# A decoder step in split fp32: activations, gains, first-stage weights and cached keys handed over in the layouts that the kernel used to make with transposes

## The chip, the cores and the metric

One core of one Trainium2 chip runs one launch of one program. The time is the device time of a launch in microseconds (us); for this kernel a change of more than 0.2% (about 4.3 us) can be told from no change.

## What is computed

The reference is one inference step of a two-layer decoder trunk over 1024 prompt tokens and 64 sample tokens (8 sequences of 8), model width 1024, all in fp32. The part around the change:

```
def gmlp_mixer(h, n, w_in, ln_g, ln_b, w_s, b_s, w_out):   # h = rms_norm(x, sg_norm_pre)
    z = jax.nn.gelu(h @ w_in, approximate=False)
    u, v = jnp.split(z, 2, axis=-1)
    v = layer_norm(v, ln_g, ln_b)
    vc = v.reshape(B, S // n, n, SGU_GROUPS, SGU_GROUP_DIM)
    w = jnp.where(causal, w_s[:, :n, :n], 0.0)              # causal token weights, per group
    mixed = jnp.einsum('gts,bcsgd->bctgd', w, vc) + b_s[:, :n].T[:, :, None]
    y = u * mixed.reshape(B, S, SGU_WIDTH)
    return y @ w_out, v_rows
...
x = x + rms_norm(out, norm_post)                            # then a SwiGLU FFN of width 2816
...
kk = jnp.concatenate([cache_k, k_new], axis=1)              # layer 2, sample tokens: 128 cached keys each
scores = jnp.einsum('btkgd,bskd->bkgts', qg, kk)            # 16 query heads on 2 key heads, window 128, sinks
```

Layer 1 is the gated mixer and its FFN; layer 2 is sliding-window attention (prompt and sample tokens) and its FFN.

## The kernel before

Features lie on the 128 partitions and tokens on the free axis. The 1088 tokens are cut into three chunks, CH = 384, 384 and 320 columns; the 1024 features into KD = 8 tiles. Each fp32 operand is held as two halves, a rounded high part (ACT writes it) and the remainder (DVE subtracts), and a product is three matmuls, high*high, high*low and low*high (`chain`, L636 to L638): 8 tiles of the contraction by 3, 24 matmuls for one output tile and chunk.

The first stage computes v = gelu(h @ w_in[:, 1024:]), 8 weight column tiles by 3 chunks. It works as follows. SP loads x in 9 blocks of 128 tokens by rows (L583), two weight tiles into the two `raw` buffers (L472), and 14 gain and bias vectors of 8 rows each into one tile (L599). TensorE transposes every block feature tile by feature tile into PSUM (`prep_x`, L702, 72 transposes of 128x128 or 128x64), ACT and DVE split the result into the x pairs (L642, L643). The vectors are turned by two transposes (L612, L618). A weight tile is multiplied by the gain of the norm on DVE (L512, for the first tile piecewise on ACT and DVE, L518, L519), then split (L396, L397). `scale_x` squares the rows of x and sums them on ACT (L711), DVE and POOL make rsqrt of the mean (L714, L715), TensorE turns it into a row over partitions (L720), DVE copies it (L722, `srow`). A chain's result stays in one of 5 PSUM banks until the `srow` of its chunk is there (`sgate`); then DVE multiplies (L768) and ACT takes gelu (L769) into the tile `vT[d]`, POOL adds up over the features (L773). Chains of tiles d = 0, 1, 2 go first, chunk by chunk as x arrives; from d = 3 on they run tile by tile. I write (d, c) for the chain of weight tile d and chunk c.

Later stages: the causal token weights `sg_w_s` are loaded by rows, cut with a select on POOL (L820, L822) and turned on TensorE (`token_weights`, L830, L834; 8 and 8 transposes, ACT copies them out). In the attention, `Samples` loads the cached keys of a key head by rows into a `raw` buffer (L309), turns them in 8 transposes (L324) and copies them out on ACT (L326), twice.

The program is written in an order which a scheduler turns into one queue per engine; `flow` is a list of work to be written later, by a count of TensorE time. ACT and DVE are held to the written order in the first stage (`manual_schedule`). All loads wait in the one queue of SP, with at most 8 in flight, and a load into a `raw` buffer waits until DVE has read the tile before it.

## Time and profile before

| | |
|---|---|
| median of 3 runs | 2127.33 us (2126.31 to 2130.13) |
| the profiled execution, its own time | 2133.59 us |
| its span, first to last instruction | 2131.6 us |
| TensorE busy in the span | 98% |
| VectorE, ScalarE, GpSimd busy | 64%, 49%, 8% |
| mean granted TensorE clock | 0.995 of full |

The profiled execution took 6.3 us longer than the median of the runs, and 2.0 us of its time lie outside its span. TensorE is PE in the profile, VectorE DVE, ScalarE ACT, GpSimd POOL; SP issues the loads. A row of a timeline is the start in us, the length, the engine, line, operation, output and inputs, and in brackets the idle time before it and what ended that.

### The profile page before, as it was taken

Reading aid. Unit: us, or ns where it says so; the run is one execution under the profiler, and the core shown is the slowest. Engines: PE = TensorE matmul, PEld = TensorE weight load, DVE = VectorE, ACT = ScalarE, POOL = GpSimd, SP = SyncE. Lnnn points to the kernel's source line nnn. Section 1 sums busy time; section 2 is a strip of 40 time slices with the busy share of each in tenths; the row PEclk is TensorE's granted clock in tenths of the full one; section 3 lists DMA queues with packets and bytes.
Section 4 is the critical chain, followed back from the end, with each engine's and each line's share of the span. In section 5 each row is a group of like instructions: output and inputs, shape, how many; then the busy total and the mean of one; then the engine's idle time right before and its main releaser. Section 6 shows DMA issues by size and latency. Waiting matters only on the chain.

```text
span 2131.6 us, 29327 instructions
## 1 busy us (share of the span) xinstructions
PE 2098.7 (98%) x10996; PEld 1797.8 (84%) x10996; DVE 1370.7 (64%) x2205; ACT 1048.1 (49%) x2112; POOL 167.1 (8%) x226
## 2 busy tenths in 40 slices
PE   7999999999999999999999999999999999999998
PEld 6999988888888888888799887788888888888886
DVE  5456558666666666567767776486566656665676
ACT  5234547544444443434567675565444444444342
POOL 0422211000000000000013221010000000000000
PEclk9999999999999999999999999999999999999999
DMA  4211134232323237757342111332222333277574
GB/s 137 70 40 37 55 112 137 76 100 81 102 95 100 81 101 256 282 169 257 113 146 59 48 46 54 106 127 81 90 92 91 99 96 93 81 264 269 177 256 148
DMA packets 176723, 257.10 MB, mean 121 GB/s; under 512 B 24659, under 2 KB 104773, under 8 KB 176582
## 3 DMA queue, kind: packets, MB, share of 16 engines
q1 hardware_dynamic: 176582, 255.24, 37.1%
q8 instruction: 86, 1.41, 0.3%
q14 instruction: 55, 0.45, 0.1%
HBM read 188.96 MB, written 60.62 MB: 117 GB/s over the span
## 4 chain that ended last, share of the span: by engine, by line
PE 93%; DVE 4%; ACT 2%; DMA 1%; issue 0%; POOL 0%; SPq 0%; DVEq 0%; POOLq 0%; ACTq 0%
PE bank L1614 15%; PE bank L1388 13%; PE bank L1389 13%; PE bank L1390 13%; PE bank L636 5%; PE bank L638 5%; PE bank L637 5%; PE aux L1614 4%; PE bank L1020 3%; PE bank L1022 3%; PE bank L1021 3%; PE bank L1468 2%; PE bank L1467 2%; PE aux L1622 2%; PE aux L1121 1%; PE aux L2359 1%
## 5 line engine op out<-in xcount | busy, mean ns | idle before, releaser
L1388 PE MATMUL bank<-act,act 128*128 128x512 f32 x1232 | 485.0, 394 | 2.3 <-ACT act L1796 2.3
L1389 PE MATMUL bank<-act,act 128*128 128x512 f32 x1232 | 482.4, 392 | 0.0
L1390 PE MATMUL bank<-act,act 128*128 128x512 f32 x1232 | 479.7, 390 | 0.0
L1614 PE MATMUL bank<-act,act 128*128 128x512 f32 x1452 | 341.2, 389 | 0.0
L1614 PEld LDWEIGHTS bank<-act,act 128*128 128x128 f32 x1452 | 272.4, 188 | 56.5
L397 DVE TENSOR_TENSOR act<-raw,act 128x1024 fp32r<-128x1024 f32 x189 | 233.4, 1236 | 126.4 <-ACT act L396 117.3
L396 ACT ACTIVATE act<-raw 128x1024 fp32r<-128x1024 f32 x189 | 199.8, 1058 | 205.1 <-PE bank L1468 71.1
L1390 PEld LDWEIGHTS bank<-act,act 128*128 128x128 f32 x1232 | 231.4, 188 | 49.0
L1388 PEld LDWEIGHTS bank<-act,act 128*128 128x128 f32 x1232 | 231.6, 188 | 48.2 <-ACT act L1796 3.1
L1389 PEld LDWEIGHTS bank<-act,act 128*128 128x128 f32 x1232 | 231.8, 188 | 43.4
L642 ACT ACTIVATE act<-act 128x1024 fp32r<-128x1024 f32 (+4 forms) x183 | 152.7, 882 | 174.2 <-PE bank L1614 65.8
L636 PE MATMUL bank<-act,act 128*128 128x384 f32 (+1 forms) x624 | 210.9, 338 | 1.4 <-DVE act L768 1.4
L638 PE MATMUL bank<-act,act 128*128 128x384 f32 (+1 forms) x624 | 207.7, 333 | 0.3 <-DVE act L397 0.3
L637 PE MATMUL bank<-act,act 128*128 128x384 f32 (+1 forms) x624 | 206.7, 331 | 0.7 <-DVE tok L993 0.7
L643 DVE TENSOR_TENSOR act<-act,act 128x1024 fp32r<-128x1024 f32 (+4 forms) x183 | 176.6, 1005 | 35.0 <-ACT act L642 24.4
L480 ACT ACTIVATE raw<-raw,vcol 128x256 f32<-128x256 f32 x352 | 152.0, 498 | 70.3 <-DMA raw<-in_f_w_up 50.8
L998 POOL TENSOR_TENSOR tok<-tok,expo 128x1 f32<-128x1 f32 (+1 forms) x63 | 39.0, 619 | 1594.0 <-DVE tok L993 1593.9
L636 PEld LDWEIGHTS bank<-act,act 128*128 128x128 f32 x624 | 119.0, 191 | 3.6 <-DVE act L768 1.6
L637 PEld LDWEIGHTS bank<-act,act 128*128 128x128 f32 x624 | 119.0, 191 | 1.5 <-DVE tok L993 1.0
L638 PEld LDWEIGHTS bank<-act,act 128*128 128x128 f32 x624 | 118.8, 190 | 1.5 <-issue 0.9
L1020 PE MATMUL bank<-act,act 128*128 128x512 f32 x256 | 102.3, 402 | 0.8 <-ACT act L396 0.4
L1021 PE MATMUL bank<-act,act 128*128 128x512 f32 x256 | 100.9, 395 | 0.0
(298 smaller groups left out, 3160.1 us busy)
## 6 DMA issues: line engine op xcount, KB each, us to landing
act<-in_f_w_down SPq DMA_DIRECT2D x90, 512.0 KB
raw<-in_f_w_gate SPq DMA_DIRECT2D x44, 512.0 KB
raw<-in_f_w_up SPq DMA_DIRECT2D x44, 512.0 KB
act<-hid_s SPq DMA_DIRECT2D x40, 512.0 KB
rows<-stream SPq DMA_DIRECT2D x24, 512.0 KB
hid_x<-rows SPq DMA_DIRECT2D x44, 256.0 KB
hid_s<-act SPq DMA_DIRECT2D x44, 256.0 KB
hid_s<-rows SPq DMA_DIRECT2D x44, 256.0 KB
```

Of the source, the lines that this page charges most:

```text
L396: nc.scalar.activation(self.hi, raw, AF.Copy)
L397: nc.vector.tensor_tensor(self.lo, raw, self.hi.bitcast(F32), op=ALU.subtract)
L636: nc.tensor.matmul(out[:, :n], h, xh[:, cs:cs + n], start=begin, stop=False)
L637: nc.tensor.matmul(out[:, :n], h, xl[:, cs:cs + n], start=False, stop=False)
L638: nc.tensor.matmul(out[:, :n], l, xh[:, cs:cs + n], start=False, stop=end)
L643: nc.vector.tensor_tensor(lo, src, hi.bitcast(F32), op=ALU.subtract)
L1020: nc.tensor.matmul(ps[:m, :], xh, h, start=begins and j == 0, stop=False)
L1021: nc.tensor.matmul(ps[:m, :], xl, h, start=False, stop=False)
L1388: nc.tensor.matmul(ps, h, xh, start=begin and k == 0, stop=False, skip_group_check=not begin)
L1389: nc.tensor.matmul(ps, h, xl, start=False, stop=False, skip_group_check=not begin)
L1390: nc.tensor.matmul(ps, l, xh, start=False, stop=k == 3, skip_group_check=not begin)
L1614: nc.tensor.matmul(ps, x, w, start=begin and e == k == 0, stop=end and e == n - 1 and k == 2, skip_group_check=adds)
```

## The change

All five edits are in the data's layout and in the code that follows from it. The host hands over more arrays, laid out anew (`laid_out`): x by feature (`x_turned`, 1024 by 1088), `sg_w_in` as 16 column tiles that are contiguous per partition, the vectors as columns (`columns`, 128 by 106), the token weights and cached keys turned.

1. `prep_x` has no transposes: x_turned is loaded into the tiles `vT[d]` in pieces of 384 or 320 columns, and split from there. `scale_x` still needs x by rows, so x is loaded a second time; the squares overwrite it.
2. The vectors are one load; no transposes.
3. The token weights are loaded turned, and POOL's selects work on the turned tile.
4. The cached keys are loaded turned, straight into their slot, by two loads at `enter`; no `raw` buffer, no transposes, no copy.
5. The first stage has a written order that includes SP's queue: tiles d = 0 and 1 both use the piecewise preparation, interleaved with the splits of chunk 0 and chunk 1; (0, 1) and (1, 0) are written k by k together (`v_chains`); the weight tiles d = 2 and 3 are loaded into two free activation tiles (`W.first(apool)`), so that four weight tiles are on their way before a buffer comes free.

```diff
         def enter(self, slot, kc, v):
...
+            for r in range(2):
+                nc.sync.dma_start(self.kc[r * HD:(r + 1) * HD, :DB * P], a["cache_k_turned"][kv])
...
-            for hb in range(2):
-                ps = aux()
-                for b in range(4 * hb, 4 * hb + 4):
-                    nc.tensor.transpose(ps[:, b % 4 * P:(b % 4 + 1) * P], self.raw[:, b * P:(b + 1) * P], ident)
-                flow.pe(400)
-                nc.scalar.activation(self.kc[:, hb * 512:(hb + 1) * 512], ps, AF.Copy)
...
+        def first(self, pool):
+            self.raws.append(pool)
+            self.load()
...
+    def load_part(c, ds=range(KD)):
+        cs, n = CH[c]
+        for d in ds:
+            nc.sync.dma_start(vT[d][:, cs:cs + n], a["x_turned"][d * P:(d + 1) * P, cs:cs + n])
+
+    nc.sync.dma_start(vcol, a["columns"])
+    load_part(0, range(4))
+    W.first(rpool)
+    load_part(0, range(4, KD))
+    W.first(rpool)
+    load_part(1)
     for b in range(3):
         load_x(b)
...
+    W.first(apool)
+    load_part(2)
+    for b in range(3, 6):
+        load_x(b)
+    W.first(apool)
...
     def prep_x(c, ds=range(KD)):
         cs, n = CH[c]
-        blocks = blocks_of(c)
         for d in ds:
-            ps = aux()
-            for j, (b, m) in enumerate(blocks):
-                nc.tensor.transpose(ps[:, j * P:j * P + m], xt[b][:m, d * P:(d + 1) * P], ident[:m, :m])
-            split(x[d][0][:, cs:cs + n], x[d][1][:, cs:cs + n], ps[:, :n])
-        flow.pe(3 * len(ds) * 120)
+            split(*(t[:, cs:cs + n] for t in (*x[d], vT[d])))
...
+    def v_chains(*some):
+
+        pss = [bank() for _ in some]
+        for k in range(KD) if len(some) > 1 else [None]:
+            for ps, (d, c, w) in zip(pss, some):
+                chain(ps, w, x, *CH[c], **({} if k is None else dict(ks=[k], begins=k == 0, ends=k == KD - 1)))
+        for ps, (d, c, w) in zip(pss, some):
+            v_end(ps, d, c)
...
+    with tc.manual_schedule(engines={mybir.EngineType.Activation, mybir.EngineType.DVE, mybir.EngineType.SP}):
+        prep_x(0, [0])
+        W.prepare(1, lambda j: j < 7 and prep_x(0, [j + 1]))
         ww = [W.get()]
         v_chain(0, 0, ww[0])
+        W.prepare(1, lambda j: prep_x(1, [j]))
+        ww.append(W.get())
+        v_chains((0, 1, ww[0]), (1, 0, ww[1]))
+        scale_x(0)
+        v_chain(1, 1, ww[1])
         W.prepare(1)
         ww.append(W.get())
...
+        flow.run()
+        prep_x(2)
+        for b in range(6, NB + 1):
+            last_x = load_x(b)
+        scale_x(1)
         v_chain(2, 0, ww[2])
...
+        v_chain(0, 2, ww[0])
+        W.done(ww[0])
+        flow.run()
+        v_chain(2, 1, ww[2])
+        last_power = scale_x(2)
+        v_chain(1, 2, ww[1])
+        W.done(ww[1])
+        v_chain(2, 2, ww[2])
...
-    def token_weights(i):
-        ps = aux()
-        if i < 2:
-            for g in range(4 * i, 4 * i + 4):
-                nc.tensor.transpose(ps[:, (g % 4) * P:(g % 4 + 1) * P], ws[:, g, :], ident)
...
+    with tc.issue_after(last_x.ins):
+        nc.sync.dma_start(wsT, a["sg_w_s_turned"])
```

How the queues change. TensorE, where the first chain runs; `bank` tiles are a chain's output, `aux_` the transposes'. In the kernel before, near its start:

```order
L702 MATMUL aux_203<-ident_71,act_95 128x128
L702 MATMUL aux_203<-ident_71,act_96 128x128
L702 MATMUL aux_203<-ident_71,act_97 128x128
L636 MATMUL bank_241<-act_139,act_191 128x384
L637 MATMUL bank_241<-act_140,act_191 128x384
L702 MATMUL aux_211<-ident_71,act_95 128x128
L702 MATMUL aux_211<-ident_71,act_96 128x128
L702 MATMUL aux_211<-ident_71,act_97 128x128
L638 MATMUL bank_241<-act_139,act_192 128x384
```

In the changed kernel, the same engine, from the end of its first chain (0, 0) on (bank_213; bank_274 is (0, 1), bank_275 is (1, 0), bank_331 is (1, 1)):

```order
L628 MATMUL bank_213<-act_110,act_179 128x384
L629 MATMUL bank_213<-act_111,act_179 128x384
L628 MATMUL bank_274<-act_96,act_179 128x384
L628 MATMUL bank_275<-act_96,act_238 128x384
L629 MATMUL bank_275<-act_97,act_238 128x384
L628 MATMUL bank_331<-act_96,act_238 128x384
L630 MATMUL bank_213<-act_110,act_180 128x384
L630 MATMUL bank_275<-act_96,act_239 128x384
L628 MATMUL bank_275<-act_98,act_238 128x384
L629 MATMUL bank_275<-act_99,act_238 128x384
```

The chains are no longer cut by transposes, and three of them advance together with each new split of chunk 1. L628 to L630 are the lines L636 to L638 of before.

SP, where x by rows stands. In the kernel before, from the start (act_ tiles are blocks of x):

```order
L599 DMA tmp_106<-in_sg_norm_pre 8x128
L583 DMA act_95<-in_x_prompt 128x1024
L583 DMA act_96<-in_x_prompt 128x1024
L583 DMA act_97<-in_x_prompt 128x1024
L472 DMA raw_111<-in_sg_w_in 128x8x128
L472 DMA raw_113<-in_sg_w_in 128x8x128
L599 DMA tmp_105<-in_sg_norm_pre 8x128
```

In the changed kernel, after the columns, chunks 0 and 1 of x_turned (16 loads) and the weight tiles d = 0 and 1:

```order
L599 DMA act_118<-in_x_turned 128x384
L599 DMA act_119<-in_x_turned 128x384
L586 DMA act_143<-in_x_prompt 128x1024
L586 DMA act_145<-in_x_prompt 128x1024
L586 DMA act_147<-in_x_prompt 128x1024
L477 DMA act_149<-in_sg_w_in_tiles 128x1024
L599 DMA act_112<-in_x_turned 128x320
```

The rows of x, first in the queue before, now stand behind 19 loads, and the weight tile d = 2 right behind the first three of them.

DVE, behind the splits of chunk 1. In the kernel before (L643 splits x, L512 and L397 prepare a weight tile, L714 the mean):

```order
L643 TENSOR_TENSOR act_154<-aux_340,act_153 128x384
L512 TENSOR_TENSOR raw_239<-raw_239,vcol_27_137 128x1024
L397 TENSOR_TENSOR act_372<-raw_239,act_371 128x1024
L619 COPY vcol_104<-aux_403 128x106
L714 TENSOR_SCALAR col_412<-ssq_158 128x3
L643 TENSOR_TENSOR act_140<-aux_416,act_139 128x320
```

In the changed kernel (L635 splits x, L699 the mean, L515 and L391 the weight tile d = 2, L707 the scale row, L763 the evacuation of a chain):

```order
L635 TENSOR_TENSOR act_111<-act_119,act_110 128x384
L699 TENSOR_SCALAR col_327<-ssq_170 128x3
L515 TENSOR_TENSOR act_149<-act_149,vcol_95 128x1024
L391 TENSOR_TENSOR act_357<-act_149,act_356 128x1024
L707 COPY srow_47_167<-aux_361 128x384
L763 TENSOR_TENSOR act_112<-bank_213,srow_47_167 128x384
L763 TENSOR_TENSOR act_113<-bank_275,srow_47_167 128x384
L635 TENSOR_TENSOR act_97<-act_112,act_96 128x320
```

The mean of chunk 0 now stands ahead of weight tile d = 2, and the evacuations of chunk 0 ahead of the splits of chunk 2, which come into the columns of the same vT tiles.

## Rows read from the trace of the kernel before

**Rows 1.** The page's chain that ended last, by engine.
```profile
PE 93%; DVE 4%; ACT 2%; DMA 1%; issue 0%; POOL 0%; SPq 0%; DVEq 0%; POOLq 0%; ACTq 0%
```
**Rows 2.** Windows: bounds, length, busy time by engine, PEclk, DMA share, GB/s.
```profile
0.00:4.86 4.86, 0.24 (x1) 0.18 (x2) 0.79 (x5) 1.49 (x2) 2.21 (x14) 1.00 0.51 158
4.86:8.00 3.14, 1.80 (x6) 1.00 (x6) 0.00 (x0) 0.00 (x0) 0.00 (x0) 1.00 0.97 350
8.00:11.00 3.00, 1.70 (x7) 1.30 (x8) 1.41 (x4) 1.66 (x4) 0.00 (x0) 1.00 1.17 304
11.00:13.00 2.00, 2.00 (x10) 1.90 (x9) 1.67 (x6) 1.45 (x4) 0.00 (x0) 1.00 1.02 396
13.00:16.00 3.00, 2.65 (x18) 2.31 (x16) 2.38 (x7) 2.62 (x8) 0.00 (x0) 1.00 0.87 253
16.00:20.00 4.00, 3.75 (x23) 3.40 (x23) 2.87 (x6) 2.32 (x6) 0.00 (x0) 1.00 0.94 296
```
**Rows 3.** Timeline of TensorE: first transposes, spacing inside chains, start of (3, 0).
```profile
4.86 0.90 PE L702 MATMUL aux<-ident,act 128*128 128x128 f32 x3 [2.29 <-DMA act<-in_x_prompt]
6.20 0.90 PE L702 MATMUL aux<-ident,act 128*128 128x128 f32 x3 [0.44 <-DMA act<-in_x_prompt]
8.55 0.90 PE L702 MATMUL aux<-ident,act 128*128 128x128 f32 x3 [1.45 <-DMA act<-in_x_prompt]
...
21.68 0.33 PE L636 MATMUL bank<-act,act 128*128 128x384 f32 x1
...
22.55 0.33 PE L638 MATMUL bank<-act,act 128*128 128x384 f32 x1
...
66.67 0.31 PE L638 MATMUL bank<-act,act 128*128 128x320 f32 x1
...
67.26 0.34 PE L636 MATMUL bank<-act,act 128*128 128x384 f32 x1
```
**Rows 4.** Windows as in rows 2: three of the first stage, a later one.
```profile
30.27:33.60 3.33, 3.33 (x15) 3.14 (x14) 2.01 (x5) 0.98 (x2) 0.00 (x0) 0.51 0.00 0
44.38:50.26 5.88, 4.46 (x25) 2.56 (x23) 4.40 (x10) 4.59 (x10) 0.00 (x0) 1.00 0.00 0
50.94:54.14 3.20, 3.20 (x12) 3.20 (x11) 2.43 (x5) 3.20 (x8) 1.82 (x3) 0.50 0.03 8
186.00:300.00 114.00, 114.00 (x690) 105.48 (x690) 55.54 (x130) 56.90 (x143) 24.96 (x32) 1.00 0.23 71
```
**Rows 5.** Groups by line and form: count, busy us, mean ns, idle before.
```profile
L397 DVE TENSOR_TENSOR act<-raw,act 128x1024 fp32r<-128x1024 f32 x189 | 233.4, 1236 | 126.4 <-ACT act L396 117.3
L711 ACT ACTIVATE act<-act 128x1024 f32<-128x1024 f32 x8 | 8.3, 1047 | 0.0
L396 ACT ACTIVATE act<-raw 128x1024 fp32r<-128x1024 f32 x5 | 5.3, 1057 | 6.6 <-DVE raw L512 6.6
L769 ACT ACTIVATE act<-act 128x384 f32<-128x384 f32 x6 | 2.7, 518 | 1.5 <-DVE act L768 1.5
L518 ACT ACTIVATE act<-raw,vcol 128x128 fp32r<-128x128 f32 x8 | 3.0, 393 | 0.1
```
**Rows 6.** Timeline of ACT: three L518 directly behind each other.
```profile
15.33 0.97 ACT L518 ACTIVATE act<-raw,vcol 128x128 fp32r<-128x128 f32 x3
```
**Rows 7.** Timeline of TensorE: transposes inside chains, and what follows them.
```profile
87.45 0.60 PE L830 MATMUL aux<-ident,act 128*128 128x128 f32 x4
87.80 0.39 PE L636 MATMUL bank<-act,act 128*128 128x320 f32 x1
...
1129.88 1.04 PE L324 MATMUL aux<-ident,raw 128*128 128x128 f32 x8
1130.67 0.42 PE L636 MATMUL bank<-act,act 128*128 128x384 f32 x1
```
**Rows 8.** Windows as in rows 2: two 512 KB weight loads; the attention's last part.
```profile
22.00:28.20 6.20, 5.02 (x33) 4.67 (x31) 0.00 (x0) 1.25 (x3) 0.00 (x0) 1.00 0.61 172
1250.00:1300.00 50.00, 47.05 (x418) 40.29 (x416) 42.54 (x123) 36.83 (x145) 10.42 (x9) 1.00 0.15 46
```

More of the change, by code (lines that the diff above doesn't have):

```diff
@@ L302, in __init__ @@
             self.kv = kv
-        def load(self, raw):
-            self.raw = raw
-            t = raw.rearrange("p (b r d) -> p b r d", b=DB, r=2)
-            for r in range(2):
-                nc.sync.dma_start(t[:, :, r], a["cache_k"][:, :, self.kv].rearrange("b j d -> j b d"))
         def enter(self, slot, kc, v):
@@ L437, in add, with add_turned @@
             self.todo.append(Entry("tile", k, [(0, k, n, src)], gain))
+        def add_turned(self, src, parts, gain):
+            m = KD // parts
+            self.todo.append(Entry("tile", KD, [(i * m * P, m, P, src[:, i * m:(i + 1) * m]) for i in range(parts)], gain))
         def add_rows(self, w, ks, h):
@@ L525, in prepare @@
                     self.named[e.key] = u
-                if e.kind != "base":
+                if e.kind != "base" and raw[1] is not apool:
                     self.raws.append(raw[1])
@@ L602, in trunk_kernel @@
+    x = [act_pair() for _ in range(KD)]
+    vT = [act_tile() for _ in range(KD)]
+    def load_part(c, ds=range(KD)):
[8 more added lines that the diff above has]
+    load_part(1)
     for b in range(3):
         load_x(b)
-    W.load()
-    for i, (name, k) in enumerate(vecs):
-        r0, n = gain[(name, k or 0)]
-        load_vec(vrow[r0:r0 + n, :], name, k)
-        if i % 2 and 3 + i // 2 <= NB:
-            load_x(3 + i // 2)
@@ L687, in scale_rows @@
         return [special([P, CH[c][1]], f"srow{c}") for c in range(3)]
-    x = [act_pair() for _ in range(KD)]
     srow = scale_rows()
@@ L754, in block @@
             return self.at(f, b * P, P if b < NB else NS)
-    vT = [act_tile() for _ in range(KD)]
     msum = [special([P, CW], "sum", bufs=4) for _ in CH]
@@ L776, in v_chain @@
         sgate[c].then(evac)
-    with tc.manual_schedule(engines={mybir.EngineType.Activation, mybir.EngineType.DVE}):
-        prep_x(0, range(3))
-        W.prepare(1, lambda j: j < 5 and prep_x(0, [j + 3]))
+    with tc.manual_schedule(engines={mybir.EngineType.Activation, mybir.EngineType.DVE, mybir.EngineType.SP}):
+        prep_x(0, [0])
+        W.prepare(1, lambda j: j < 7 and prep_x(0, [j + 1]))
         ww = [W.get()]
         v_chain(0, 0, ww[0])
+        W.prepare(1, lambda j: prep_x(1, [j]))
[3 more added lines that the diff above has]
+        v_chain(1, 1, ww[1])
@@ L784, in trunk_kernel @@
         W.prepare(1)
         ww.append(W.get())
-        v_chain(1, 0, ww[1])
-        prep_x(1)
-        v_chain(0, 1, ww[0])
-        W.prepare(1)
-        ww.append(W.get())
-        v_chain(2, 0, ww[2])
-        all_vecs()
-        scale_x(0)
-        prep_x(2)
-        v_chain(1, 1, ww[1])
-    for c in range(1, 3):
-        if c == 1:
-            scale_x(1)
-        for d in range(3):
-            if c == 2 or d == 2:
-                v_chain(d, c, ww[d])
-            if d == 2 and c < 2:
-                scale_x(c + 1)
-            if c == 2:
-                W.done(ww[d])
-            flow.run()
@@ L837, in trunk_kernel @@
     window_masks()
-    for i in range(3):
-        flow.later(K["tokw"] + 2000 * i, lambda i=i: token_weights(i))
     for d in range(3, KD):
@@ L2439, with laid_out @@
          ('k_sample', (8, 8, 2, 64)), ('v_sample', (8, 8, 2, 64))]
+def laid_out(np, inputs):
+    x = np.concatenate([inputs["x_prompt"].reshape(SEQ, D), inputs["x_sample"].reshape(NS, D)])
+    vecs = [inputs[name] if i is None else inputs[name][i] for name, i in VECS]
+    new = {"x_turned": x.T,
+           "columns": np.concatenate([np.reshape(v, (-1, P)) for v in vecs]).T,
+           "sg_w_in_tiles": inputs["sg_w_in"][0].reshape(KD, P, 2 * KD, P).transpose(2, 1, 0, 3),
+           "sg_w_s_turned": inputs["sg_w_s"][0].transpose(2, 0, 1),
+           "cache_k_turned": inputs["cache_k"].transpose(2, 3, 0, 1).reshape(2, HD, DB * P)}
+    return {**{name: inputs[name] for name in _INS}, **new}
 def kernel(**inputs):
```

107 lines of the change are left out of this document (41 added, 66 removed).

## The prediction

> **What bounds the kernel now.** I read the page first: the chain that ended last is 93% TensorE [rows 1], and TensorE is busy for 98% of the span. So only two things count: TensorE instructions that vanish, and the few places where TensorE waits. The windows say where those are. In the later stages TensorE has no gap: 114.00 of 114.00 us between 186 and 300 us [rows 4]. The gaps lie at the start, so next I read the first stage. Its start is a relay: blocks of x land at 4.86, 6.20 and 8.55 us, and TensorE, ready for them, waits each time [rows 3]. Then chains and transposes alternate, and the chain of the first weight tile without a share in this, (3, 0), starts at 67.26 us [rows 3]. Ahead of it stand nine chains. Inside a chain, five steps take 22.55 - 21.68 = 0.87 us, 0.174 us each, and with 320 columns four steps take 67.26 - 66.67 = 0.59 us, 0.148 us each [rows 3]. A chain is 24 steps: 4.18 us, or 3.54 us. Six of one and three of the other are 35.7 us of the 67.26. The other 31.6 us are transposes, waits, and two stretches in which the granted clock stood at half, 1.2 instead of 2.4 GHz: 0.51 and 0.50 for 3.33 and 3.20 us [rows 4], about 1.6 us lost in each. This is what the change can reach; I take (3, 0) as the mark, because its place and all that follows it is the same in both programs.
>
> **The new first stage: when do the loads land?** The old start shows what the loads do when many are in flight. By its windows, 4.86 us at 158 GB/s, 3.14 at 350, 3.00 at 304, 2.00 at 396, 3.00 at 253 and 4.00 at 296 [rows 2] add up to 0.77, 1.87, 2.78, 3.57, 4.33 and 5.51 MB by 4.86, 8, 11, 13, 16 and 20 us. Blocks of x (0.52 MB each, first in the queue) landed at 4.86, 6.20 and 8.55 us [rows 3], when 0.77, 1.24 and 2.03 MB had been moved, 0.2 to 0.5 MB more than they and what stood ahead: a load lands when 0.3 MB beyond its own end have been moved. Now SP's new queue, summed up from the diff: half of weight tile 0 ends at 1.10 MB, chunk 0 of x_turned at 2.15, weight tile 1 at 2.68, chunk 1 at 4.25, three blocks by rows at 5.82, weight tile 2 at 6.35, chunk 2 at 7.66, three more blocks at 9.23, weight tile 3 at 9.75 MB. With 0.3 MB added, and 296 GB/s beyond 20 us, they land at 6.7, 9.9, 11.5, 16.7, 22.0, 23.8, 28.2, 33.6 and 35.3 us.
>
> **The chain of work on these loads.** ACT alternates: scale a piece of weight tile 0, split a feature tile of x. The pair costs 0.393 + 0.518 = 0.91 us by means [rows 5], but back to back instructions overlap: three L518 take 0.97 us, 0.32 each [rows 6], so the pair can be as short as 0.74; I take 0.8. The first piece is done at 6.7 + 0.4 = 7.1 us, seven more pairs at 12.7 us, and (0, 0) ends with them, a little over 13. Its pace is ACT's, not TensorE's: 24 steps want 4.18 us and get about 6. Then the same pairs make weight tile 1 and chunk 1, whose pieces have landed in time. From 13.6 us on each new piece feeds 9 steps (three chains), 1.57 us of TensorE for 0.8 us of ACT, so TensorE is the bound again: 73 steps, 12.7 us, to 26.3 us.
>
> Then the gate. The last of the three row blocks lands at 22.0, its square takes 1.05 us more (L711 [rows 5]); with the small steps behind it I put DVE's mean at 23.4, ahead of weight tile 2, which lands at 23.8: two DVE passes of 1.24 us and one of ACT of 1.06 [rows 5] make it ready at 27.3 us. TensorE, with three row transposes (0.3), has come to its first low half at about 26.9: a wait of 0.4 us, the one new wait on the path. (2, 0) ends at 31.2 us. Behind it, chunk 2's splits need the evacuation of chunk 0, because x_turned and v share tiles; DVE copies srow at 27.8, evacuates two chains by 28.9, and ACT's eight splits end at about 33.5, while TensorE has (2, 1) to do in between. Weight tile 3 is prepared by about 41 us and used at 46, and its evacuations free the bank of (2, 2) at 42.1, under a microsecond ahead of TensorE. So (0, 2), (2, 1), (1, 2), (2, 2) run through: 14.8 us and 0.3 of row transposes, 46.3 us; with 0.2 for small waits, (3, 0) starts at 46.5 us. **Gain: 67.26 - 46.5 = 20.8 us.** The second copy of x costs nothing here, as long as it hides behind the chains: if not, the bound below prices it.
>
> Bounds. With ACT's pair at 0.74 us and no wait: 45.4 us, a gain of 21.8. At the other end stands the load rate. x_turned has lines of 1.5 KB; before has lines of 4 KB (x) and 0.5 KB (weights). The worst row of weight loads is 172 GB/s [rows 8], in a window in part idle. At that rate each MB of x_turned takes 2.5 us longer than at 300: weight tile 2 lands 7.8 us later and is ready at 35.1, weight tile 3 lands at 46.3 and is ready at 49.8, two evacuations and (2, 2) later (3, 0) starts at 54.4: a gain of 12.8. I stay near the upper end, since the old start, half a mix of these lines, holds 253 to 396 GB/s. The Trainium skill speaks against the change here: DMA: Bandwidth & Descriptors, Bandwidth, has 138 GB/s for a load of 64 KB and 341 for 1 MB, and advises loads of 1 MiB; x_turned comes in 24 loads of 164 and 197 KB, and an estimate between its figures, some 200 GB/s, would give nearly the lower gain. The trace does not bear that out for 512 KB with several in flight (350 GB/s [rows 2]); no row has such small ones.
>
> The clock. After the stretch up to 50.26 us, in which TensorE did mostly transposes and was busy for 4.46 of 5.88 us, the granted clock fell to 0.50 [rows 4]. The new stage has no such stretch and no wait of this size, so I count no fall; if the 0.4 us wait grows to over 1 us and brings one, it costs 1.6 us. The Trainium skill (TensorE: Matmul & The Clock Gate, Part 4: PE-mode transpose) says that transposes do not count as work for the clock; the trace agrees with that stretch, and by that rule even a wait in the new stage has less to add to.
>
> **The other edits.** Token weights: four transposes move the chain by 87.80 - 87.45 = 0.35 us [rows 7]; eight are 0.70, the eight small ones at most that, I take 0.6: 1.3 us, in a stretch where TensorE never waits. ACT's copies and POOL's selects (the same count) lie beside chains; SP's load of them waits for TensorE to be done with weight tile 0, and the weight tile behind it is wanted only from about 90 us on (d = 7). Cached keys: eight transposes move the chain by 1130.67 - 1129.88 = 0.79 us [rows 7], twice: 1.6 us. Their loads now go out at `enter`, well ahead of the scores that read them, with whole chains between; if that cover were gone, a load would show as a wait of a few us. The vectors' transposes lie in the first stage and are in its sum. In the attention the scheduler shuffles TensorE's queue (its rows differ only here and in the first stage), and TensorE idles there anyway, 2.95 us of the last 50 [rows 8]: it may lose this or double it. I count 0 and keep +-3.
>
> **Sum.** 20.8 + 1.3 + 1.6 = 23.7 us. The profiled execution would take 2133.59 - 23.7 = 2109.9 (span 2107.9); it stood 6.3 us above the median, so the median is 2127.33 - 23.7 = 2103.6, say **2104 us**.
>
> **Rivals.**
> *Small lines are slow.* The load rate near 172 GB/s for x_turned, a gain between 12.8 and 19, with the rest 16 to 22 in all: 2106 to 2112 us. For it speaks that no row has 1.5 KB lines, against it the mean of the old mix.
> *More than counted.* The attention's idle time goes as well: 21.8 + 2.9 + 3 = 27.7 us, 2099.6 us.
> *The head start is given back.* The chains go ahead, but a gate behind them does not (POOL's sums, the norm over v): only 2.9 us stay, 2124.4 us, no change by the measure. Against it: POOL is busy for 24.96 of 114 us later, and TensorE waits for nobody [rows 4].
> *Slower: the double x starves the stage.* If all loads ran slowly, (3, 0) would start 8.1 us after weight tile 3 lands (3.5 to prepare, 1.1 to evacuate, 3.5 for (2, 2)). To be 4.3 us slower with the 2.9 saved elsewhere, it has to land after 66.4 us: 10.05 MB in 64 us, below 157 GB/s. At 130 GB/s: 2127.3 + 17.7 = 2145 us. The rows at hand lie above that.
>
> **How the numbers follow.** The forecast (2100 to 2108 us) 0.72; small lines, beyond 2108, 0.13; more than counted 0.08; given back 0.04; slower 0.03. The range reaches from the best sum, 2099, to the worst row for the loads with the attention a little worse, 2113; outside lie about 0.15. A change of over 0.2% (4.3 us) can be told from none: faster 0.93, same 0.04, slower 0.03.
>
> **What the profile would show.** Right: (0, 0) from about 7 to 13 us with short gaps, three chains without gaps to about 26, (3, 0) at 46 to 47, no stretch of half clock between 13 and 46, no L324 or L830. A wait of TensorE near 27 us on DVE's low half of weight tile 2 shows its size. Wrong: splits waiting for x_turned beyond 17 us (slow lines), squares waiting for rows (the second copy), or a wait in 1150 to 1300 us well above before.

## The result, and the profile after

| | before | after |
|---|---|---|
| median of the runs | 2127.15 us (6 runs, 2126.25 to 2132.14) | 2111.91 us (6 runs, 2110.69 to 2116.10) |
| the profiled execution, its own time | 2133.59 us | 2110.69 us |
| its span | 2131.6 us | 2108.8 us |
| mean granted TensorE clock | 0.995 | 0.997 |

The ratio is 0.9926, 95% interval 0.9913 to 0.9940: 0.74% faster, 15.2 us by the medians. The forecast was 2104 us, so 8 us of its gain are missing in the median, though the two profiled executions differ by 22.8 us of span and 22.9 us of own time, nearly the 23.7 us forecast; the section on the prediction says why that is partly luck. The page after still has TensorE as the bound; the chain that ended last [rows 1] stays TensorE's.

```profile
PE 2079.5 (99%) x10890; PEld 1783.4 (85%) x10890; DVE 1362.5 (65%) x2209; ACT 1047.3 (50%) x2112; POOL 171.6 (8%) x225
...
PE 92%; DVE 3%; ACT 2%; DMA 1%; issue 1%; POOL 0%; SPq 0%; DVEq 0%; POOLq 0%; ACTq 0%
```

The windows of the changed kernel's first stage (busy time of each engine, then the clock, the DMA share and GB/s), to be held against [rows 2]:

```profile
0.00:4.86 4.86, 0.00 (x0) 0.00 (x0) 1.04 (x5) 2.01 (x3) 2.16 (x14) 1.00 0.50 136
4.86:8.00 3.14, 0.00 (x0) 0.00 (x0) 0.22 (x1) 0.00 (x0) 0.00 (x0) 1.00 0.96 307
8.00:11.00 3.00, 2.12 (x7) 2.13 (x8) 2.08 (x6) 2.58 (x8) 0.00 (x0) 1.00 1.06 388
...
16.00:20.00 4.00, 4.00 (x25) 4.00 (x24) 4.00 (x12) 4.00 (x11) 0.00 (x0) 1.00 0.95 352
20.00:28.00 8.00, 8.00 (x48) 8.00 (x47) 2.85 (x4) 3.61 (x7) 1.77 (x1) 1.00 1.03 374
28.00:36.00 8.00, 8.00 (x50) 7.96 (x49) 5.56 (x11) 6.18 (x15) 1.52 (x2) 1.00 0.94 329
```

Two things matter here: from 16 us on TensorE is busy all the time (4.00 of 4.00 us, then 8.00 of 8.00), and from 4.86 us on the loads run at 307 to 388 GB/s. The waits of TensorE in the first 48 us are one row, the wait for the first piece:

```profile
PE bank L628 <- ACT act L521: 8.9, 1, 8.9
```

TensorE's timeline, at the places that answer to [rows 3], the start of the first chain, the middle of it, and (3, 0):

```profile
8.88 0.69 PE L628 MATMUL bank<-act,act 128*128 128x384 f32 x1 [8.88 <-ACT act L521]
9.36 0.52 PE L629 MATMUL bank<-act,act 128*128 128x384 f32 x1
...
13.84 0.52 PE L628 MATMUL bank<-act,act 128*128 128x384 f32 x1
14.16 0.41 PE L629 MATMUL bank<-act,act 128*128 128x384 f32 x1
14.41 0.33 PE L630 MATMUL bank<-act,act 128*128 128x384 f32 x1
14.59 0.33 PE L628 MATMUL bank<-act,act 128*128 128x384 f32 x1
...
47.56 0.31 PE L630 MATMUL bank<-act,act 128*128 128x320 f32 x1
47.71 0.34 PE L628 MATMUL bank<-act,act 128*128 128x384 f32 x1
```

The first chain starts at 8.88 us and its steps are 0.32 us apart, 384 columns at 1.2 GHz, until 14.2 us; from 14.4 us on they are 0.17 us apart. (The clock column has 1.00 there; the step is what shows the level.) (3, 0) starts at 47.71 us, against 67.26 [rows 3]: 19.55 us. ACT's row says what the first chain waited for:

```profile
3.97 0.52 ACT L634 ACTIVATE act<-act 128x384 fp32r<-128x384 f32 x1 [1.67 <-DMA act<-in_x_turned]
8.42 0.40 ACT L521 ACTIVATE act<-raw,vcol 128x128 fp32r<-128x128 f32 x1 [3.93 <-DMA act<-in_x_turned]
8.73 0.51 ACT L634 ACTIVATE act<-act 128x384 fp32r<-128x384 f32 x1
9.14 0.39 ACT L521 ACTIVATE act<-raw,vcol 128x128 fp32r<-128x128 f32 x1
```

The first piece of x_turned was there at 3.97 us, the first half of weight tile 0 only at 8.4. (The row puts the wait down to x_turned; that it was the weights is read from the program, since the instruction reads the weight tile.) A pair of ACT's instructions, one for the weights and one for x, takes 0.71 us (8.42 to 9.14 and on).

### The profile page after: what moved, and what is told of

Same layout as the page of the kernel before. It is cut to its first block, busy times and chain, and to the rows that moved or that the text cites. A ratio compares the mean times of both kernels' runs of the same rounds, so it can differ in the third digit from the quotient of the medians.

```text
span 2108.8 us, 29128 instructions
## 1 busy us (share of the span) xinstructions
PE 2079.5 (99%) x10890; PEld 1783.4 (85%) x10890; DVE 1362.5 (65%) x2209; ACT 1047.3 (50%) x2112; POOL 171.6 (8%) x225
## 4 chain that ended last, share of the span: by engine, by line
PE 92%; DVE 3%; ACT 2%; DMA 1%; issue 1%; POOL 0%; SPq 0%; DVEq 0%; POOLq 0%; ACTq 0%
PE bank L1593 14%; PE bank L1367 13%; PE bank L1368 13%; PE bank L1369 13%; PE bank L628 5%; PE bank L629 4%; PE bank L630 4%; PE aux L1593 4%; PE bank L1001 3%; PE bank L999 3%; PE bank L1000 3%; PE bank L1447 2%; PE bank L1446 2%; PE aux L1601 2%; PE aux L1100 1%; PE aux L2336 1%
## 5 line engine op out<-in xcount | busy, mean ns | idle before, releaser
L391 DVE TENSOR_TENSOR act<-raw,act 128x1024 fp32r<-128x1024 f32 x186 | 228.1, 1230 | 121.1 <-ACT act L390 111.4
L634 ACT ACTIVATE act<-act 128x1024 fp32r<-128x1024 f32 (+5 forms) x207 | 164.0, 836 | 173.8 <-PE aux L1593 62.9
L628 PE MATMUL bank<-act,act 128*128 128x384 f32 (+1 forms) x624 | 208.8, 335 | 9.4 <-ACT act L521 8.9
L635 DVE TENSOR_TENSOR act<-act,act 128x1024 fp32r<-128x1024 f32 (+5 forms) x207 | 190.7, 959 | 36.0 <-ACT act L634 24.9
L630 PE MATMUL bank<-act,act 128*128 128x384 f32 (+1 forms) x624 | 205.7, 330 | 0.0
L628 PEld LDWEIGHTS bank<-act,act 128*128 128x128 f32 x624 | 118.0, 189 | 10.9 <-ACT act L521 8.9
L630 PEld LDWEIGHTS bank<-act,act 128*128 128x128 f32 x624 | 117.9, 189 | 0.8 <-issue 0.7
```

What stands on the lines that cost most here:

```text
L391: nc.vector.tensor_tensor(self.lo, raw, self.hi.bitcast(F32), op=ALU.subtract)
L628: nc.tensor.matmul(out[:, :n], h, xh[:, cs:cs + n], start=begin, stop=False)
L630: nc.tensor.matmul(out[:, :n], l, xh[:, cs:cs + n], start=False, stop=end)
L635: nc.vector.tensor_tensor(lo, src, hi.bitcast(F32), op=ALU.subtract)
```

## The experiments

**Both kernels again.** Four runs without an edit, to see what the first profiles were draws of.

> The kernel before, unchanged, with clock and span of every run. The forecast took 23.7 us off the profiled execution of before (2133.59 us, granted clock 0.995) and carried them to the median one-to-one; the profiles differ by 22.8 us of span, the medians by 15.2 us. Theory A: the profiled execution of before was a draw with more stretches at half clock than usual (it shows four before its last 50 us: near 31, 51, 1065 and 1310 us; each costs 1.6 us). Then the typical run of before shows a mean clock of 0.997 or 0.998 and a span of 2124 to 2126 us, and if this profile is such a run, at least two of those stretches are missing. Theory B: the stretches belong to the program and come in every run; then the clock is 0.995 in all runs, this profile shows the same four, and the 6 us lie elsewhere. Time: 2127 us, ratio 1.000.

> The changed kernel, unchanged. By theory A its profiled execution (2110.69 us, the fastest of six) was a draw with few half-clock stretches; the median is again near 2112 us, runs spread over 2110 to 2116 with 1.5 to 2 us for each 0.001 of the mean clock, and the new profile has one or two such stretches more than the first. Ratio to before 0.9925 to 0.993. If the ratio comes out near 0.989 (2104 us), the first measurement was the odd one and the forecast was right.

> One more profiled execution of the kernel before, to see which of its half-clock stretches come every time. Two so far: the first (2133.59 us) has stretches near 31, 51, 1065 and 1305 us and its chain (3, 0) at 67.26 us; the second (2126.49 us) has one near 1296 us and (3, 0) at 63.33 us. Theory A (a draw): neither of the two early stretches is bound to come; without them (3, 0) lies at 63 to 64 us, with one at about 65, with both at about 67; the own time is 2124.5 us plus 1.6 us for each stretch beyond the second's one, plus the scatter of a microsecond. Theory B (the second execution was the odd one): both early stretches are there and (3, 0) is at 67.

The kernel before: 2129.28 us (11 runs, 2126.01 to 2133.13), ratio to its other runs 1.0003 (0.9994 to 1.0013). Its profiled execution took 2126.49 us, span 2124.4, clock 0.998. In the two stretches of [rows 4] in which the first execution had 0.51 and 0.50, its windows read:

```profile
30.27:33.60 3.33, 3.03 (x19) 2.37 (x17) 1.91 (x4) 1.57 (x3) 0.00 (x0) 1.00 0.00 0
50.94:54.14 3.20, 3.20 (x23) 3.20 (x22) 1.97 (x3) 2.55 (x5) 3.11 (x4) 1.00 0.50 143
```

and its (3, 0):

```profile
63.33 0.34 PE L636 MATMUL bank<-act,act 128*128 128x384 f32 x1
```

The third profiled execution (2127.92 us, one run) has the later of the two stretches and not the earlier:

```profile
30.00:35.00 5.00, 4.70 (x28) 4.08 (x27) 2.85 (x4) 3.52 (x6) 0.00 (x0) 1.00 0.01 4
45.00:55.00 10.00, 8.60 (x43) 8.39 (x44) 7.08 (x12) 7.54 (x14) 5.99 (x7) 0.83 0.19 56
```

```profile
63.90 0.34 PE L636 MATMUL bank<-act,act 128*128 128x384 f32 x1
```

So the same program starts (3, 0) at 67.26, 63.33 and 63.90 us. The wait ahead of the later stretch is there each time: 1.36 us on L768, until 50.26, 47.90 and 46.91 us. The half clock behind it comes in the first and the third; from the end of that wait to (3, 0) it is 17.00, 15.43 and 16.99 us, so the stretch costs 1.6 us. The wait ahead of the earlier stretch is not the same each time. Here it is in the first, the second and the third execution:

```profile
29.97 0.59 PE L702 MATMUL aux<-ident,act 128*128 128x128 f32 x3 [2.94 <-DVE act L643]
28.77 0.55 PE L702 MATMUL aux<-ident,act 128*128 128x128 f32 x3 [1.20 <-DVE act L643]
27.79 0.55 PE L702 MATMUL aux<-ident,act 128*128 128x128 f32 x3 [1.08 <-DVE act L643]
```

In the first, DVE started on weight tile 2 at 28.22 us, in the others at 27.01 and 26.05, and its splits of x stand behind that. So the first execution was 1.2 and 2.2 us late before its first stretch of half clock began. From this row to the wait on L768 it took another 1.2 us longer than either. Of the 3.9 us to the second execution, late loads are then 1.2 and half clock 2.7 (1.2 and 1.6); of the 3.4 us to the third they are 2.2 and 1.2.

Theory A holds in kind: the stretches come and go, and the execution that the forecast was worked out from was a draw near the slow end, above every one of the other six times of its table. Its numbers do not hold: the eleven runs have a median clock of 0.996 and a median span of 2127.3 us, not 0.997 or 0.998 and 2124 to 2126. The second and third executions are 2.8 and 1.6 us faster than the medians of the runs beside them, so they are draws too, on the other side.

The changed kernel again: 2112.08 us, ratio 0.9922 (0.9908 to 0.9937); its (3, 0) lies at 46.80 us, with the first chain from 8.16 us on and its steps of 0.32 us only until 12.9. Behind the first stage its profile has three stretches of half clock (near 1046, 1227 and 1280 us), the first one had two (near 1278 and 1315): 0.9 us ahead at (3, 0), it is 0.8 us longer at the end, 1.7 us for the one stretch more.

> The changed kernel once more, beside the next two on the same chip. Median 2110.5 to 2113 us, ratio 0.9915 to 0.993, (3, 0) at 46 to 47.7 us, the first chain half its steps or more at 0.32 us. A ratio of 0.990 or less (what the forecast wanted) would say that the two earlier measurements were both off.

2112.91 us, 0.9921 (0.9908 to 0.9934), first chain from 8.74, steps of 0.32 until 14.7, (3, 0) at 47.86. Three measurements of the ratio agree, 0.9926, 0.9922, 0.9921; the forecast's 2103.6 / 2127.33 = 0.989 lies outside of each interval.

**Warm TensorE ahead of the first chain.**

```diff
+    ps = aux()
+    for j in range(56):
+        nc.tensor.matmul(ps[:, :P], identr, identr, start=True, stop=True)
     with tc.manual_schedule(...):
         prep_x(0, [0])
```

> The changed kernel with 56 small matmuls of the identity by itself ahead of the first chain, into a PSUM buffer nobody reads, in the time in which TensorE waits for the first loads. In the changed kernel the chain (0, 0) starts at 8.88 us and goes in steps of 0.32 us, twice the full-clock step, until 14.2 us. Theory: TensorE paced that chain because it was at half clock; warm, ACT's pairs (0.71 us) pace it, it ends at about 14.6 instead of 16.1 us, and (3, 0) starts at 46.2 to 46.5 instead of 47.7 us: 1.2 to 1.5 us faster (2110.5). Rival: the half clock was covered by ACT or by the loads behind (weight tile 1, chunk 1), and the mark moves by less than 0.4 us.

2116.17 us, ratio 0.9942 (0.9928 to 0.9955), 4.1 us slower than the changed kernel of the same chip. The filling was longer than the hole:

```profile
2.37 12.21 PE L776 MATMUL aux<-ident 128*128 128x128 f32 x56 [2.37 <-POOL ident L250]
14.37 0.63 PE L628 MATMUL bank<-act,act 128*128 128x384 f32 x1
14.80 0.52 PE L629 MATMUL bank<-act,act 128*128 128x384 f32 x1
...
18.64 0.44 PE L629 MATMUL bank<-act,act 128*128 128x384 f32 x1
18.91 0.34 PE L630 MATMUL bank<-act,act 128*128 128x384 f32 x1
```

The 56 took 0.218 us each and held the first chain up to 14.4 us, from 8.2 to 8.9 in the changed kernel; (3, 0) came at 52.73, 4.9 to 5.9 us late: most of what TensorE loses at its start is lost for good. And 12 us of them left the clock at the lower level, since the chain behind still steps by 0.32 us until 18.6. So the theory itself was not put to the test.

With 17 matmuls of the chain's own width it is otherwise:

```diff
+    wide = identr[:, None, :].to_broadcast([P, 3, P])
+    for j in range(17):
+        nc.tensor.matmul(ps[:, :3 * P].rearrange("p (a b) -> p a b", a=3), identr, wide, start=True, stop=True)
```

> The changed kernel with 17 matmuls of the identity by three copies of itself side by side (384 columns, the width of the chains) ahead of the first chain, where TensorE waits for loads; the result is read by nobody. The same try with 56 matmuls of 128 columns ran 0.213 us each, so that they ended at 14.4 us, held the first chain up by 5.5 us and cost 4.1 us, and the first chain behind them still went in steps of 0.32 us for 4.3 us. If 384 columns take 0.32 us as in the chain, these 17 end at about 7.9 us, ahead of the first piece (8.1 to 8.9 us). Theory: wide matmuls bring the granted clock up before the chain starts; (0, 0) goes at ACT's pace, and (3, 0) starts 0.8 to 1.5 us earlier than in the changed kernel's three executions (46.1 to 47.7 us), at 45.0 to 46.0. Rival: only the real operands bring it up, or the stage is paced by the loads: the mark stays at 46 to 47.7. Time 2110.5 to 2112 us.

```profile
2.36 4.85 PE L777 MATMUL aux<-ident 128*128 128x384 f32 x17 [2.36 <-POOL ident L250]
8.08 0.45 PE L628 MATMUL bank<-act,act 128*128 128x384 f32 x1 [0.87 <-ACT act L521]
8.36 0.34 PE L629 MATMUL bank<-act,act 128*128 128x384 f32 x1
8.54 0.36 PE L630 MATMUL bank<-act,act 128*128 128x384 f32 x1
8.79 0.44 PE L628 MATMUL bank<-act,act 128*128 128x384 f32 x1
```

No step of 0.32 us is left; three steps now take 0.73 us, ACT's pair. The first step of the second weight tile comes at 13.76 us (14.55 and 15.45 in the first two profiles of the changed kernel), (3, 0) at 46.14, and the median is 2109.57 us, 0.9904 (0.9890 to 0.9919). The mark misses the theory's 45.0 to 46.0 us and lies at the early end of the rival's 46 to 47.7. By the mark 0.7 to 1.7 us were half clock; but an execution in which the lower level ended early (at 11.2 us, below) reaches 46.13 without any warming. The wider matmuls differ from the small ones in more than their number of columns (time per matmul, reuse of the weights), so which of these the clock follows stays open.

**An earlier start.**

```diff
-    load_part(0, range(4))
-    W.first(rpool)
-    load_part(0, range(4, KD))
+    W.first(rpool, lambda i: load_part(0, [2 * i, 2 * i + 1]))
     W.first(rpool)
...
-        W.add_turned(a["sg_w_in_tiles"][KD + d], 1 + (d < 2), ("sg_norm_pre", 0))
+        W.add_turned(a["sg_w_in_tiles"][KD + d], (4, 2, 1)[min(d, 2)], ("sg_norm_pre", 0))
```

The function handed to `W.first` is called behind each part of weight tile 0 (`first` and `load` hand it on; these lines are left out above).

> The changed kernel with the start of SP's queue in another order: weight tile 0 in four parts of two feature tiles, each followed by the two pieces of x_turned that go with it (before: four pieces of x, half of the weights, four pieces, the other half). The changed kernel waits until 8.1 to 8.9 us for the first half of the weights, although it needs an eighth of it and one piece of x. Theory: the stage is TensorE's from its first matmul on (holding the start up by 5.5 us had cost 4.1 to 5), so an earlier start is kept nearly whole: first matmul at 5.0 to 5.8 us, (3, 0) 2.0 to 3.0 us earlier (44 to 45 us), less up to 0.6 us for weight tile 2, which was ready 2.1 us ahead; time 2109 to 2110 us. Rival: the loads of chunk 1 or the three row blocks pace the stage behind the first chain; then (3, 0) moves by less than 1 us.

> Both: the queue's start in the new order, and 8 matmuls of 384 columns on the identity ahead of the first chain (2.4 to about 5 us). If both theories hold, the start is 2.5 us earlier and half the half-clock stretch lies in the wait: (3, 0) at 43.5 to 44.5 us, 0.5 to 1 us ahead of the kernel with the order alone; 2108.5 us. If a wait for weight tile 2 (a microsecond at most) or for the row blocks takes over, it stays at the time of the kernel with the order alone.

One thing in the first of these expectations is not so: in the changed kernel both halves of weight tile 0 stand together behind the first four pieces of x, not one behind each four. The start moved as expected, to 5.62 us, and the rest did not follow: (3, 0) at 46.29 instead of 44 to 45, median 2109.50 us, 0.9906 (0.9892 to 0.9921). That the median lies within the expected 2109 to 2110 us is luck, since the mark does not. The waits of TensorE up to 48 us:

```profile
PE bank L627 <- ACT act L522: 5.8, 2, 5.6
PE bank L627 <- ACT act L633: 0.8, 1, 0.8
```

and ACT's row behind the second:

```profile
13.34 0.52 ACT L633 ACTIVATE act<-act 128x384 fp32r<-128x384 f32 x1 [1.05 <-DMA act<-in_x_turned]
```

It waits for chunk 1's first piece. Rival and theory each hold in part: up to about 13 us the start was bound by the queue's order, behind it by the bytes. With 8 warming matmuls as well: 2108.65 us, 0.9898 (0.9882 to 0.9915), (3, 0) at 46.81 instead of 43.5 to 44.5, not earlier (the median is again near the expected 2108.5, and again not for its reason); ACT waited for x_turned at 11.50 and 13.85 us, and the first chain stepped by 0.32 us until 10.3. In all these profiles (3, 0) follows the first step of the second weight tile by 32.3 to 32.4 us (13.76 to 46.14, 13.91 to 46.29, 14.55 to 46.80): from there on the stage is TensorE's alone. That points to a chain that needs fewer bytes next:

```diff
-        W.prepare(1, lambda j: prep_x(1, [j]))
+        W.prepare(1, lambda j: None)
         ww.append(W.get())
-        v_chains((0, 1, ww[0]), (1, 0, ww[1]))
+        v_chain(1, 0, ww[1])
+        prep_x(1)
+        v_chain(0, 1, ww[0])
         scale_x(0)
         v_chain(1, 1, ww[1])
-        W.prepare(1)
+        W.prepare(1, lambda j: None)
```

> The kernel with the queue's start in the new order and 8 warming matmuls (2108.65 us), with the chain (1, 0) ahead of the ones that need chunk 1, and weight tile 2 prepared piece by piece. In that kernel ACT waited 1.54 and 0.54 us for pieces of x_turned and TensorE 0.92 and 0.58; (1, 0) needs weight tile 1 alone, 0.52 MB, where the chains now there need 0.2 to 1.6 MB of chunk 1 behind it. In all five profiled executions of the new stage (3, 0) starts 32.3 to 32.4 us after the second weight tile's first step; theory: that step moves from 13.8 to 14.6 us to about 12.8 to 13.4, (3, 0) to 45.1 to 45.8, 0.7 to 1.2 us earlier than with the other order (46.3 to 46.8); time 2107.5 to 2108.5. Rival: weight tile 2 or the row blocks, ready at 26.3 and 24.6 us in any order, take over as the bound and the 32.4 us grow by as much; (3, 0) at 46.2 or later.

2106.58 us, 0.9895 (0.9879 to 0.9910), the fastest kernel of the study, 6.3 us ahead of the changed kernel on the same chip (2112.91). Its waits and its mark:

```profile
PE aux L776 <- POOL ident L250: 2.4, 1, 2.4
PE bank L627 <- ACT act L522: 0.6, 1, 0.6
```

```profile
45.52 0.34 PE L627 MATMUL bank<-act,act 128*128 128x384 f32 x1
```

The second weight tile starts at 12.75 us, so (3, 0) should be at 45.1; it is 0.4 later, within the expectation. By the mark the version gains 1.3 to 2.3 us on the changed kernel, by the profiled spans 2.7 (2108.5 to 2105.8 us). The rest of the 6.3 us lies behind the first stage, where the programs are the same; the granted clock of its runs was 0.995 to 0.998, that of the changed kernel's beside it 0.995 to 0.997, half of them at 0.995. So I take 2 to 3 us as the version's own, an estimate. Against the kernel with the new order and 8 warming matmuls alone, the ratios do not show a gain (0.9895 and 0.9898, measured on two chips); the mark does, 46.81 to 45.52.

**One part undone: the column tiles.**

```diff
-        W.add_turned(a["sg_w_in_tiles"][KD + d], 1 + (d < 2), ("sg_norm_pre", 0))
+        W.add_lines(w_in[:, D + d * P:D + (d + 1) * P], 1 + (d < 2), ("sg_norm_pre", 0))
...
```

> The changed kernel without the part of the change that cuts sg_w_in into column tiles: the 16 weight tiles of the first stage are loaded from the array as it was, in lines of 512 bytes instead of 2 to 4 KB; all else is as changed. Theory: with eight loads in flight the line does not set the rate (355 to 395 GB/s with lines of 1.5 KB in this stage), so (3, 0) stays within 46.1 to 47.7 us and the time within 0.1% of the changed kernel. Rival, the small lines are slow: at the 172 GB/s of [rows 8] each tile of 0.52 MB takes 1.5 us longer; the first half of tile 0 is 0.8 us later, weight tile 2, with three tiles at or ahead of it, 4.5 us later, of which 2.1 us are covered; (3, 0) at 49 to 50 us, 2 to 3 us slower.

2110.65 us, 0.9916 (0.9902 to 0.9930), against 2112.91 of the changed kernel; (3, 0) at 46.13, earlier than in the three executions of that kernel (46.80 to 47.86), with steps of 0.32 us from 8.08 to only 11.1. Its loads are as fast as those of the changed kernel (352 and 374 GB/s in the same windows):

```profile
16.00:20.00 4.00, 4.00 (x25) 4.00 (x24) 3.53 (x10) 4.00 (x11) 0.00 (x0) 1.00 1.04 389
20.00:28.00 8.00, 8.00 (x49) 7.96 (x48) 3.53 (x5) 2.81 (x5) 0.87 (x1) 1.00 1.07 362
```

Lines of 512 bytes cost nothing here: this part of the change brings nothing that shows, and the rival of the slow lines falls.

**The other two edits.** With the new first stage and the old token weights and cached keys:

```diff
-        nc.sync.dma_start(wsT, a["sg_w_s_turned"])
+    nc.sync.dma_start(ws, a["sg_w_s"][0].rearrange("g t s -> t g s"))
...
+    for i in range(3):
+        flow.later(K["tokw"] + 2000 * i, lambda i=i: token_weights(i))
...
-                nc.sync.dma_start(self.kc[r * HD:(r + 1) * HD, :DB * P], a["cache_k_turned"][kv])
...
+                    nc.tensor.transpose(ps[:, b % 4 * P:(b % 4 + 1) * P], self.raw[:, b * P:(b + 1) * P], ident)
```

> The new first stage alone: the causal token weights and the cached keys are again loaded by rows and turned on TensorE as in the kernel before (16 and 16 transposes, their copies on ACT, selects on POOL). By the forecast these cost 1.3 and 1.6 us: 2.9 us slower than the changed kernel (2114.8 us), of it 1.3 us between the mark (3, 0) and the token mixing, 1.6 us in the attention. By the marks of the two profiles it is 1.0 us for the token weights, and between 1086 and 1297 us 2.2 to 2.6 us. Rival: transposes in the attention fall into TensorE's idle time there; then 1.3 us or less.

2113.18 us, 0.9928 (0.9915 to 0.9941): 1.1 us slower, less than the spread of its five runs (2110.92 to 2114.30). By marks, from (3, 0) to the first matmul of the layer norm's sums (`stat_cols`, which the expectations call the token mixing; nothing of the change but the token weights lies between), it takes 111.8 - 46.08 = 65.7 us, the changed kernel 111.8 - 47.71 = 64.1, the kernel before 132.4 - 67.26 = 65.1: the token weights are worth 1.0 to 1.6 us. Now the opposite half: the same lines the other way round, from the kernel before, its first stage as it was.

> The other half: the kernel before with its first stage as it was, and only the token weights and the cached keys handed over turned. The forecast has 1.3 and 1.6 us for these, 2.9 us off the kernel before, ratio 0.9986. What the marks of the executions so far say: between (3, 0) and the token mixing the three executions of before take 65.1 to 65.2 us, all with the new token weights 64.1, so 1.05 us. Between the first instructions of the attention and its last the three of before take 219.7 to 221.3 us, eight of the changed kernel and its variants 219.3 to 221.0, although eight transposes fewer stand there twice; each of the eight has two half-clock stretches in it (near 1220, 1277 or 1315 us), the later two of before one (near 1297). Theory: the transposes are saved, and a second stretch at half clock gives 1.6 us back; then this kernel too has two stretches there, 219.3 to 221 us, and is 1.0 us faster than before in all, ratio 0.9995. Rival: the second stretch comes with the new first stage, by where the loads stand; then it has one, 218.0 to 218.5 us, and the kernel is 2.7 us faster, 0.9987. (3, 0) starts at 63.3 to 64 us, or 1.6 to 3.9 later if a half-clock stretch falls in the first stage, as in the first of the three executions of before.

2136.62 us, ratio 1.0041 (1.0027 to 1.0055): 8.4 us slower than before, which neither theory had. SP's queue, DVE and TensorE show why:

```profile
17.63 5.86 SPq L806 DMA_DIRECT2D wbT<-in_sg_w_s_turned  x8
23.53 0.92 SPq L871 DMA_DIRECT2D bs<-in_sg_b_s  x2
24.55 1.00 SPq L459 DMA_DIRECT2D raw<-in_sg_w_in  x2
...
32.05 1.22 DVE L498 TENSOR_TENSOR raw<-raw,vcol 128x1024 f32<-128x1024 f32 x1 [10.81 <-DMA raw<-in_sg_w_in]
...
33.80 0.90 PE L690 MATMUL aux<-ident,act 128*128 128x128 f32 x3 [7.23 <-DVE act L631]
```

The eight tiny loads of the sample tokens' weights (8 by 64 numbers each) wait only for the last load of x, so in my mixture the scheduler put them ahead of weight tile 2. They hold the queue for 5.86 us. DVE has that tile at 32.05 us instead of 26.05 to 28.22 (the three executions of before), and TensorE, which waited 1.08 to 2.94 us for the split behind it, now waits 7.23. (3, 0) starts at 71.12 us, 7.8 us later than in the second execution of before: 5.0 us stand at the end of that wait (33.80 against 28.77), and 2.8 us are two stretches of half clock behind it (near 35 and 56 us), as long as in the first execution of before. So about 5 of the 8.4 us (3.8 to 6.0, by the execution of before that it is held against) are the loads themselves. Whether the half clock comes with the long wait is not shown; the clock of the five runs was 0.993 to 0.995, that of the nine of before beside them 0.995 to 0.998. In the changed kernel the same loads go out in 10.06 us, from 31.48 us on, behind the weight tiles that are wanted next; nobody waits. So the written order of SP's queue (part 5) matters here: a forecast of 1.3 us saved would have been wrong by over 9 us for this edit.

The run still answers the other half of its question. I measure the attention from the last transpose of the value rows (L2048 of before) to the last transpose of the sample tokens' output (L380). These are windows of the third execution of the kernel before, of the second of the changed kernel, and of this mixture:

```profile
1120.00:1339.70 219.70, 213.16 (x1631) 183.44 (x1629) 160.80 (x422) 147.87 (x547) 54.89 (x59) 0.99 0.20 56
```

```profile
1102.90:1322.90 220.00, 213.85 (x1615) 183.03 (x1614) 155.19 (x422) 145.63 (x543) 55.36 (x59) 0.98 0.21 57
```

```profile
1126.80:1346.60 219.80, 213.73 (x1615) 183.01 (x1614) 154.33 (x422) 146.09 (x543) 55.04 (x59) 0.98 0.21 57
```

Sixteen transposes are gone (1631 to 1615 instructions), ACT is 2 us less busy, and the stretch is as long as it was: the clock is 0.98 instead of 0.99. The mixture has two stretches of half clock there (near 1250 and 1303 us), as the theory said, so the second does not come with the new first stage. But the kernel with the old cached keys and the new first stage has more than two as well (223.50 us, clock 0.97), so that the new cached keys bring it is not shown. The token weights bring here what they brought above: from (3, 0) to `stat_cols` it is 134.6 - 71.12 = 63.5 us, 1.6 less than in the kernel before.

## Why the prediction was right in kind and 8 us too good

*The first stage.* The mechanism was right: no transposes, no relay, TensorE without a wait from its first matmul to (3, 0). The forecast had (3, 0) at 46.5 us; it came at 47.71, 46.80 and 47.86. Of its steps, the first matmul was to come at 7.1 us and came at 8.2 to 8.9: the half of weight tile 0 landed when about 1.8 MB had been moved (136 and 307 GB/s, then 388, up to 8.4 us), 0.7 MB past its end and not 0.3. "I count no fall" of the clock held behind the first chain and missed that the first chain itself runs at the lower level, for 4.7 to 6.0 us in the changed kernel's three executions; with ACT at 0.71 us a pair, TensorE's 0.96 us for three steps was the pace until it ended, so "Its pace is ACT's" was wrong until 12.9 to 14.7 us. Against that the loads ran at 352 and 374 GB/s from 16 to 28 us instead of 296, weight tile 2 was ready 2.1 us ahead, and the wait of 0.4 us did not come. The second copy of x costs nothing, as forecast.

*The step that failed is the sum's last one, 2127.33 - 23.7 = 2103.6.* It takes a gain that was read off one execution from the median of others. The 67.26 us of that execution hold 3.4 to 3.9 us that two more executions of the same program do not: 1.2 to 2.2 us because weight tile 2 came late, 1.2 to 2.7 us of half clock. The forecast counted them among the 31.6 us of which it says "This is what the change can reach". It named the warning itself (the execution stood 6.3 us above the median) and went on. With the two other executions the term is 15.5 to 17.1 us (63.33 and 63.90, less 46.80 to 47.86) instead of 20.8. Where a run of median time starts (3, 0) is not shown. The reason that the forecast gave for a fall of the clock, the transposes ahead of it, is not enough by itself: the same transposes and the same wait of 1.36 us stand in the second execution, and no fall follows (1.00 from 50.94 to 54.14 us).

*A near hit by luck.* For the profiled execution the sum gave 2109.9 us, and 2110.69 was measured. The terms measured between these two profiles are 19.55 us at the mark, 1.0 for the token weights and 0.9 in the attention (221.3 and 220.4), 21.5 together. Most of the rest is a stretch of half clock near 1065 us, which the first execution of before has and that of the changed kernel has not.

*Token weights:* 1.3 forecast, 1.0 to 1.6 by the marks. *Cached keys:* 1.6 forecast; the transposes went, and the attention stayed at 219.3 to 221.0 us in nine executions with the new cached keys and the new first stage, against 219.7 to 221.3 in three of before. Eight of the nine have at least one half-clock stretch more than the later two of before, which fits what was given back; the ninth (the small warming matmuls) has none more and is no shorter, 220.8 us. So where the 1.6 us went stays open; the "+-3" that the forecast kept for the attention had room for it.

*The sum* is then 15.5 to 17.1, 1.0 to 1.6 and 0, together 16.5 to 18.7 us, against 15.2, 17.2 and 16.0 by medians (2127.15 - 2111.91, 2129.32 - 2112.08, 2128.86 - 2112.91).

*The rivals.* The result lies in the range of the slow lines, 2106 to 2112 us, and not for their reason: x_turned's lines of 1.5 KB came at 307 to 388 GB/s with the rest, and lines of 512 bytes changed nothing. The Trainium skill's advice for loads of 1 MiB (DMA: Bandwidth & Descriptors, Bandwidth) did not decide here either: loads of 164 to 524 KB, several in flight, ran at 307 to 388 GB/s. A slower outcome was rated by the load rate; the experiment shows the nearer danger, small loads ahead in the queue.

## What to carry to other kernels

Before a gain is read off one profiled execution, see how that execution stands among the runs: late loads and stretches of half clock that fall into the part to be removed can be a draw. Here they were 3.4 to 3.9 us that two other executions did not hold. When an early stage is cleared of waits, the next limits are the order of the queue, the bytes ahead of each first use and TensorE's low clock at its start; ask for the chain that needs the fewest bytes next. And count every DMA by its place in the queue: where eight loads of 2 KB stood ahead of one weight tile, TensorE went on 5 us later and the kernel was 8 us slower; where they stood behind it, nobody waited.

## What had not been expected of the hardware

- TensorE begins at the lower level and the moment of the rise differs from execution to execution of one program: 14.2, 12.9 and 14.7 us, with starts at 8.88, 8.16 and 8.74. The Trainium skill (TensorE: Matmul & The Clock Gate, Part 1: The HAM clock gate) says that the number of slow matmuls at the start varies from run to run of one kernel; these three agree.
- Behind 56 small matmuls, 12.2 us of them back to back, the chain still ran at the lower level; behind 17 of its own width, 4.85 us, at the higher one; behind 8 of its own width, 2.93 us, it stepped by 0.32 us until 10.3 us and, in the kernel with (1, 0) first, until 11.8.
- The clock column of the profile reads 1.00 in the first chain, where the steps are those of 1.2 GHz.
